# A decoder layer on eight cores: the order of the instructions of every engine made by a model of the engines at build time

One Trainium2 chip, all 8 NeuronCores (two dies of four). The metric is the time of one execution on the device in microseconds (us), of the slowest core. A program on all 8 cores has a second, slower state in some executions, in which the cores of one die show a lower clock. Comparisons below use the fast runs; where a slow run is named, it is called slow.

## The reference

A hybrid decoder layer: two batches of 4096 tokens, 2048 channels. Cut to what the argument touches:

```python
h = rms_norm(x, norm_gain)                       # needs the sum of squares of each token
q, k, v, z_attn, u_pool, z_pool, gates = split(einsum('bsd,de->bse', h, w_in), ...)
q = rms_norm(q.reshape(B, S, 3, 8, 128), q_norm_gain)     # one norm for each head
k = rms_norm(k.reshape(B, S, 3, 8, 128), k_norm_gain)
for g, (window, dilation) in enumerate(((128, 1), (512, 4), (2048, 16))):
    qg, kg = partial_rope(q[:, :, g], pos), partial_rope(k[:, :, g], pos)   # first 32 of 128 channels
    o_g, lse_g = dilated_window_attention(qg, kg, v[:, :, g], window, dilation)
# [cut: mix of the three groups by their softmax denominators]
# [cut: pooling mixer, two sigmoid gates, two branch products]
return x + einsum('bsd,de->bse', merged, w_out)
```

Each core does 1024 tokens of its own and the keys and values of the tokens before them that the third window reaches (the halo). The kernel has these stages: stage 1, keys and values of the third group over all those tokens, in chunks of 512; stage 2, query and key projections with the attention of 24 head-and-group units laid between them; then pooling (stage 3), gates with the branch products, and the output product.

## The kernel before

The program first calls `S.op(engine, instruction, reads, writes)` for everything. Each engine gets its instructions in the order of these calls, and semaphore waits are made from the reads and writes. An engine executes strictly in its order: **what is ready but stands behind something that waits, waits too**. So the order of the calls is the schedule. TensorE's projections are the backbone, and everything else is put in at fixed points of it:

```python
own_q, bg_q, late_q = [], [], []          # norms; attention; second halves of rotations
def tick(kc):                             # called after each of the 16 matmuls of a projection
    if kc in (3, 7, 11, 15):
        pop_own()                         # the next norm or rotation step, if there is one
    elif kc in (1, 5, 9, 13):
        pop_bg()                          # the next attention step, if its time has come

def project(banks, lhs, mov, n, reads):
    i = banks[nxt("pp", len(banks))]      # buffers go round in a fixed order
    pcount[0] += 1
    need(("ps", i))                       # flush what still uses this buffer
    # [cut]
    for kc in range(KC):
        S.op("pe", ...matmul...)
        tick(kc)
    return i
```

The steps themselves: a norm is square (ScalarE), a matmul with ones that sums over the 128 channels (TensorE), logarithm and exponential (ScalarE), product (VectorE). A rotation exchanges two halves of 16 channels by two small DMAs from SBUF to SBUF and then does three short instructions on VectorE, put in a fixed number of projections later:

```python
def rope(tag, rots, B_rots, st, B_st, c0, n, tb, B_tb, t0, after=None, wait=2):
    def swap():
        # [cut] two DMAs on SyncE's queue: rb[32:48] <- st[16:32], rb[48:64] <- st[0:16]
        def turn():
            # [cut] three VectorE instructions of 32 x n elements
        turn.due = pcount[0] + wait       # two projections later, whatever the DMA does
        late_q.append(turn)
    return swap
```

The norm of a chunk of x: 8 squares of 1024 columns (ScalarE), 7 adds and a fold (VectorE), one fp32 matmul that sums the partitions, logarithm and exponential, and 16 scalings (VectorE).

## Time and profile before

| | before |
|---|---|
| median of the first 3 runs | 1870.58 us (1868.52 to 1874.1) |
| TensorE busy | 1600.7 us, 86% of the span, 7774 matmuls |
| ends of stage 1, stage 2, stage 3 (read from the trace) | 513, 1290, 1418 us |
| share of TensorE in the chain of work that ended last | 71% |

"Busy" counts a slow matmul as busy too. So I compare with a floor: each matmul's undisturbed distance from the next (0.216 us for 512 columns, taken from the gate stage where nothing disturbs), summed. Time minus this sum is "lost". The lines of the profile are shown in the prediction and not again here. In all such lines PE is TensorE and PEld its loading of weights, DVE is VectorE, ACT ScalarE, POOL GpSimd and SP SyncE; a q behind the name marks the issue of a DMA, and L12 is line 12 of the kernel. In a list of waits the numbers are us in all, how often, and the longest.

### The profile page before, as it was taken

Reading aid. Unit: us, or ns where it says so; the run is one execution under the profiler, and the core shown is the slowest. Engines: PE = TensorE matmul, PEld = TensorE weight load, DVE = VectorE, ACT = ScalarE, POOL = GpSimd, SP = SyncE. Lnnn points to the kernel's source line nnn. Section 1 sums busy time; section 2 is a strip of 40 time slices with the busy share of each in tenths; the row PEclk is TensorE's granted clock in tenths of the full one; section 3 lists DMA queues with packets and bytes.
Section 4 is the critical chain, followed back from the end, with each engine's and each line's share of the span. In section 5 each row is a group of like instructions: output and inputs, shape, how many; then the busy total and the mean of one; then the engine's idle time right before and its main releaser. Section 6 shows DMA issues by size and latency. Waiting matters only on the chain.

```text
span 1870.6 us, 22928 instructions; the slowest of 8 cores (1861.7 to 1870.6 us)
## 1 busy us (share of the span) xinstructions
PE 1600.7 (86%) x7774; PEld 754.0 (40%) x7774; DVE 698.5 (37%) x1041; ACT 551.2 (29%) x890; POOL 76.1 (4%) x147
## 2 busy tenths in 40 slices
PE   0397778879999787778998788778999999999997
PEld 0143333324644334343453434334444444444443
DVE  2456646472100444453403544545642121112121
ACT  2235344433112444443314444443211111111000
POOL 1000000000000000000000000000000000000000
PEclk9898889889999987898999898888999999999999
DMA  9743514234454232313325323223434444444683
GB/s 202 161 135 89 147 35 123 58 91 87 87 128 66 52 84 37 73 22 79 81 46 92 76 52 74 48 40 60 91 68 75 73 78 79 79 72 76 135 225 113
DMA packets 79027, 163.06 MB, mean 87 GB/s; under 512 B 33664, under 2 KB 41728, under 8 KB 78144
## 3 DMA queue, kind: packets, MB, share of 16 engines
q0 software_dynamic: 20592, 84.42, 26.6%
q1 hardware_dynamic: 57696, 76.72, 13.8%
q8 instruction: 64, 1.05, 0.2%
q10 hardware_dynamic: 624, 0.46, 0.1%
q14 instruction: 51, 0.42, 0.1%
HBM read 220.48 MB, written 20.97 MB: 129 GB/s over the span
## 4 chain that ended last, share of the span: by engine, by line
PE 71%; DVE 10%; DMA 6%; ACT 6%; issue 5%; SPq 1%; DVEq 0%; ACTq 0%
PE ps L476 53%; PE ps L1054 6%; PE ps L1023 6%; DVE s_acc L536 3%; ACT s_sqf L534 2%; DMA s_xs_66<-xc 2%; PE ps L578 2%; DMA s_xs_60<-xc 1%; DVE s_DEN L719 1%; PE ps L798 1%; PE ps L769 1%; PE ps L547 1%; DVE s_NUM L716 1%; DVE s_hTo L557 1%; ACT s_rr_53 L583 1%
## 5 line engine op out<-in xcount | busy, mean ns | idle before, releaser
L476 PE MATMUL ps<-s_hTo,s_w_57 128*128 128x512 bf16 x3328 | 806.3, 392 | 1.1 <-ACT s_ue_115 L945 0.9
L476 PEld LDWEIGHTS ps<-s_hTo,s_w_57 128*128 128x128 bf16 x3328 | 332.4, 101 | 370.1 <-issue 31.0
L476 PE MATMUL ps<-s_hTh_55,s_w_57 128*128 128x512 bf16 (+2 forms) x640 | 116.6, 327 | 16.2 <-DVE s_hTh_55 L557 15.8
L397 POOL DMA_DIRECT2D s_w_57<-wst x136 | 72.2, 535 | 1172.7 <-PE ps L476 920.0
L476 PE MATMUL ps<-s_w_57,s_hTo 128*128 128x512 bf16 x512 | 113.6, 379 | 0.0
L1054 PE MATMUL ps<-s_mT,s_w_57 128*128 128x512 bf16 x512 | 110.7, 379 | 0.0
L536 DVE TENSOR_TENSOR s_acc<-s_acc,s_sqf 128x1024 f32<-128x1024 f32 x49 | 60.0, 1225 | 111.9 <-ACT s_sqf L534 111.9
L476 PEld LDWEIGHTS ps<-s_hTh_55,s_w_57 128*128 128x128 bf16 x640 | 56.2, 105 | 76.4 <-issue 35.4
L594 ACT ACTIVATE s_sq_50<-ps 128x512 bf16<-128x512 f32 (+1 forms) x72 | 40.3, 560 | 142.8 <-PE ps L476 142.8
L578 PE MATMUL ps<-s_sq_51,s_ones 128*128 128x512 bf16 x72 | 29.1, 404 | 59.3 <-ACT s_sq_51 L594 59.3
L476 PEld LDWEIGHTS ps<-s_w_57,s_hTo 128*128 128x128 bf16 x512 | 54.0, 106 | 54.4
L1054 PEld LDWEIGHTS ps<-s_mT,s_w_57 128*128 128x128 bf16 x512 | 50.1, 98 | 60.4
L585 DVE SCALAR_TENSOR_TENSOR s_kS_97<-ps,s_cst,s_rr_52 128x128 bf16<-128x128 f32 (+1 forms) x8 | 4.4, 551 | 173.3 <-ACT s_rr_52 L583 173.3
L476 PE MATMUL ps<-s_hTh_56,s_w_57 128*128 128x512 bf16 x256 | 64.1, 406 | 0.0
L581 ACT ACTIVATE s_rr_52<-ps 128x512 f32<-128x512 f32 (+1 forms) x72 | 40.3, 560 | 75.9 <-PE ps L578 66.3
L581 ACT ACTIVATE s_rr_53<-ps 128x512 f32<-128x512 f32 x72 | 43.1, 599 | 64.9 <-PE ps L578 54.0
L476 PE MATMUL ps<-s_w_58,s_hTh_56 128*128 128x512 bf16 x256 | 61.5, 403 | 0.0
L1023 PE MATMUL ps<-s_aT,s_w_57 128*128 128x512 bf16 x256 | 60.5, 379 | 0.0
L1023 PE MATMUL ps<-s_pT,s_w_57 128*128 128x512 bf16 x256 | 60.5, 379 | 0.0
L547 PE MATMUL ps<-s_acc,s_onesf 128*128 128x512 f32 x14 | 14.2, 1114 | 53.2 <-DVE s_acc L542 53.2
L476 PE MATMUL ps<-s_w_58,s_hTh_55 128*128 128x512 bf16 x256 | 55.9, 379 | 0.0
L476 PE MATMUL ps<-s_w_58,s_hTo 128*128 128x512 bf16 x256 | 55.6, 379 | 0.0
(319 smaller groups left out, 1576.0 us busy)
## 6 DMA issues: line engine op xcount, KB each, us to landing
s_w_57<-wst POOLq DMA_DIRECT2D x136, 512.0 KB, 5.2
s_w_57<-wst POOLq DMA_DIRECT2D x4, 2048.0 KB, 16.1
s_w_58<-wst POOLq DMA_DIRECT2D x2, 2048.0 KB, 61.3
s_xs_59<-xc SPq DMA_DIRECT2D x7, 512.0 KB, 5.2
s_xs_60<-xc SPq DMA_DIRECT2D x7, 512.0 KB, 5.3
s_xs_61<-xc SPq DMA_DIRECT2D x6, 512.0 KB, 7.7
s_xs_62<-xc SPq DMA_DIRECT2D x6, 512.0 KB, 6.3
s_xs_63<-xc SPq DMA_DIRECT2D x6, 512.0 KB, 4.4
```

Source lines behind the costliest of these rows:

```text
L397: S.op("pool", lambda g: g.dma_start(out=t[:].rearrange("p k n -> p (k n)"), in_=wst[row]), writes=bufs, dsem=f"w{i}")
L476: S.op("pe", lambda t, kc=kc, a=lhs(kc), b=mov(kc): t.matmul(ps[i][:, 0:n], lhsT=a, rhs=b, start=(kc == 0), stop=(kc == KC - 1)), reads=re ...
L534: S.op("act", lambda a: a.activation(out=sqf[:], in_=xv, func=AF.Square), reads=[B_xs[i]], writes=[B_sqf])
L536: S.op("dve", lambda v: v.tensor_tensor(out=acc[:], in0=acc[:], in1=sqf[:], op=ALU.add), reads=[B_acc, B_sqf], writes=[B_acc])
L547: S.op("pe", lambda t: t.matmul(ps[AUX][:], lhsT=onesf[:], rhs=acc[:, 0:512], start=True, stop=True), reads=[B_acc, B_onesf], writes=[B_ps ...
L557: S.op("dve", lambda v: v.scalar_tensor_tensor(out=dst(kc), in0=xs[i][:, kc % 2, :], scalar=gsc[:, kc:kc + 1], in1=rsb[ri][:], op0=ALU.mul ...
L578: S.op("pe", lambda t: t.matmul(ps[AUX][:, 0:n], lhsT=ones[:], rhs=sq[si][:, 0:n], start=True, stop=True), reads=[B_sq[si], B_ones], write ...
L581: S.op("act", lambda a: a.activation(out=rr[ri][:, 0:n], in_=ps[AUX][:, 0:n], func=AF.Ln, bias=float(128 * EPS)), reads=[B_ps[AUX]], write ...
L583: S.op("act", lambda a: a.activation(out=rr[ri][:, 0:n], in_=rr[ri][:, 0:n], func=AF.Exp, scale=-0.5), reads=[B_rr[ri]], writes=[B_rr[ri]])
L594: S.op("act", lambda a: a.activation(out=sq[si][:, 0:n], in_=ps[i][:, 0:n], func=AF.Square), reads=[B_ps[i]], writes=[B_sq[si]])
L1023: S.op("pe", lambda t, yi=yi, h=h, m=m, w=w, which=which, src=src: t.matmul(ps[yi][:], lhsT=w[:, 8 * which + h, :], rhs=src[:, h, 512 * m: ...
L1054: S.op("pe", lambda t, fi=fi, db=db, m=m, w=w: t.matmul(ps[fi][:], lhsT=w[:, db, :], rhs=mT[:, db, 512 * m:512 * m + 512], start=(db == 0) ...
```

## The change

Intent: no fixed points, and hardly any fixed turns of buffers (blocks of weights and pieces of x still go round). Each piece of work (a norm, a rotation, a bank of attention, a load) becomes a process that asks for buffers from counted pools and yields instructions, each with a duration. A discrete-event model of the five engines runs the processes at build time; when an engine is free, it takes the ready instruction with the highest priority. The sequence that comes out is frozen in the program.

The core of the diff (names kept, long runs cut):

```diff
-        own_q, bg_q, late_q = [], [], []
-        def tick(kc):
-            if kc in (3, 7, 11, 15):
-                pop_own()
-            elif kc in (1, 5, 9, 13):
-                pop_bg()
+class Flow:
+    LAT = {"pe": 0.5, "act": 0.2, "dve": 0.2, "pool": 0.3, "sp": 0.2}   # the model's us from another engine's result to its use on this one
+    RATE = 0.31e6                                                       # the model's bytes per us of large DMAs
+    def dispatch(self, eng):
+        if self.busy[eng] or not self.pend[eng]:
+            return
+        _, _, p, dur, fn, reads, writes, dma = heapq.heappop(self.pend[eng])   # by priority
+        self.S.op(eng, fn, reads=reads, writes=writes, ...)                    # the order is fixed here
+        done = self.t + dur
+        # [cut]
+        if dma is not None:
+            size = dma[0]
+            if size >= 200e3:
+                start = max(done + 1.5, self.dma_free)
+                self.dma_free = start + size / self.RATE
+                land = self.dma_free + 0.7
+            else:
+                land = done + 4.0                  # in the model a small DMA: 4 us, whatever else is under way
+def act_us(n):
+    return 0.16 + n * 0.00087
+def dve_us(n, cheap=False):
+    return 0.15 + n * (0.00053 if cheap else 0.00105)
```

```diff
-        def norm_stage(i, n, si, gcol, dst, B_dst, r=1): ...
+        def norm(i, n, gcol, dst, B_dst, r=1):
+            si = yield ("acq", P_sq)
+            yield ("op", "act", act_us(n), ...square..., [B_ps[i]], [B_sq[si]])
+            ax = yield ("acq", P_aux)
+            yield ("op", "pe", mm_us(n), ...matmul with ones..., [B_sq[si], B_ones], [B_ps[ax]])
+            F.release(P_sq, si)
+            # [cut] logarithm, exponential, product; then the buffers are released
```

Work moves as well. From the second chunk on the adds of squares go to GpSimd; the first weights wait until part of x has landed; and the late tokens that stage 2 needs are copied out of the normed chunks instead of being loaded and normed as a chunk of their own:

```diff
+                if k < 2:                                     # a load of weights
+                    yield ("wait", E_x[(0, 3 + 3 * k)])
+                    first = [B_xs[3 + 3 * k]]                 # a dependence, so a semaphore wait on the chip
+                if k == 8:                                    # the first load of value weights
+                    yield ("wait", E_x[(1, 7)])               # of the model only: no dependence
+                eng, dur = ("dve", dve_us(1024)) if c == 0 else ("pool", 2.4)     # adds of squares
+        def late_copy(c):
+            src = hTh[hi][:].rearrange("p k (r l) -> p k r l", r=4)[:, :, :, 96:128]
+            dst = hX[:, :, 0:LATE].rearrange("p k (l r) -> p k r l", r=16)[:, :, 4 * c:4 * c + 4, :]
+            yield ("op", "pool", 4.0, lambda g: g.tensor_copy(out=dst, in_=src), ...)
```

## The prediction

> **What bounds the kernel now.** I read the busy table and the slices first, then the stages, then what TensorE waited for, then single places in order of time. The slices of the page:
>
> ```profile
> PE   0397778879999787778998788778999999999997
> PEclk9898889889999987898999898888999999999999
> DMA  9743514234454232313325323223434444444683
> ```
>
> TensorE is the engine that matters, but only the right third of its row (gates, branch products, output projection) is full. The left two thirds are at 7 or 8 tenths, with a granted clock of 8 or 9 tenths. The same by stage (columns: stretch, its length, busy time and count of TensorE, weight loads, VectorE, ScalarE, GpSimd, granted clock, DMA share, GB/s):
>
> ```profile
> 0.00:43.10 43.10, 0.00 (x0) 0.00 (x0) 9.91 (x13) 9.62 (x9) 5.63 (x14) 1.00 0.95 203
> 43.10:93.00 49.90, 17.41 (x45) 5.89 (x46) 22.78 (x26) 12.88 (x16) 0.00 (x0) 0.87 0.75 165
> 93.00:513.00 420.00, 359.49 (x1547) 167.00 (x1546) 204.06 (x326) 157.93 (x237) 1.06 (x2) 0.92 0.36 95
> 589.00:900.00 311.00, 251.01 (x1300) 120.61 (x1298) 142.91 (x217) 132.81 (x228) 10.16 (x20) 0.88 0.31 61
> 980.00:1290.00 310.00, 249.32 (x1330) 121.03 (x1327) 146.95 (x224) 135.84 (x235) 14.85 (x28) 0.90 0.33 63
> 1418.00:1749.50 331.50, 331.50 (x1537) 150.29 (x1536) 66.16 (x96) 44.22 (x65) 25.45 (x48) 1.00 0.44 77
> ```
>
> The last line is the yardstick: 1537 matmuls of 512 columns in 331.5 us are 0.216 us each, no gap, full clock. I counted every matmul by width and gave each its undisturbed distance (0.216 us for 512 columns, in proportion below that, 0.03 us at least). This gives 1505 us for the whole kernel. So 366 us of 1870.6 are lost, by subtraction in each stretch: 43 before the first matmul; 38 to 93 us; 80 in the rest of stage 1 (key and value projections of all tokens, to 513 us); 191 in stage 2 (attention, 513 to 1290), of which 122 are gaps and the rest slow matmuls and short waits; 4 in the pooling stage; none in the gates; 11 at the end. In stage 2 most 512-column matmuls lie 0.22 us apart, but 174 lie 0.42 us apart, all after a gap.
>
> What TensorE waited for:
>
> ```profile
> PE ps L798 <- DVE s_E_107 L776: 70.6, 16, 7.3
> PE ps L578 <- ACT s_sq_51 L594: 59.3, 21, 8.7
> PE ps L547 <- DVE s_acc L542: 53.2, 7, 43.1
> PE ps L578 <- ACT s_sq_50 L594: 30.8, 6, 11.6
> ```
>
> These are not slow producers: VectorE and ScalarE are under half busy in the stages concerned. They stand in the wrong order. One place shows it (the first two lines VectorE, the last TensorE):
>
> ```profile
> 622.15 0.94 DVE L611 TENSOR_TENSOR s_kS_99<-s_kS_99,s_tabb 32x1536 bf16<-32x1536 bf16 x1 [4.11 <-DMA s_rotb_105<-s_kS_99]
> 625.39 0.41 DVE L776 TENSOR_TENSOR s_E_107<-s_E_107,s_msk 128x512 bf16<-128x512 bf16 x1
> 625.94 0.58 PE L798 MATMUL ps<-s_E_107,s_vS_91 128*128 128x256 bf16 x3 [7.25 <-DVE s_E_107 L776]
> ```
>
> The exponentials of this bank ended at 617.6 us. The mask multiplication (L776) stands behind a rotation that waits 4.1 us for its DMA, so TensorE waits 7.25 us for a 0.41 us instruction with ready inputs. In stage 1 it is ScalarE: squares of the next chunk, waiting for x, stand before the squares of a norm.
>
> [...]from 1420 to 1750 us all eight cores run dense at 1.00. Hence I charge a denser kernel no clock. [...]the trace shows 322 GB/s when x alone is loading (75 to 80 us).
>
> **The change part by part.** The arithmetic stays. Four things move.
>
> *1. Order.* Each piece of work is now a process that asks for buffers by count. A model with durations for each instruction issues the highest-priority ready one, and that sequence is frozen. I use none of its times, only the order that it leaves. Its durations are sound against the trace: ScalarE at 512 columns 0.605 us (trace 0.60), mask 0.42 (0.41), norm product 0.76 (0.75), rotation DMAs 4 us after issue (trace about 1.9 unobstructed, so generous). Its handoffs are too short from TensorE (0.2[...]) and too long towards it (0.5, 0.14). The chain last matmul, square, norm matmul is 1.305 us in the model[...]. Before, four matmuls (0.86 us) were put between; in the new TensorE order it is 1.3 to 1.5 us of work in most of the 96 norms of stage 2. So a norm should wait 0 to 0.3 us, not up to 9. The rotations no longer stand before ready masks, because the order counts the DMA.
>
> *2. First chunk.* Weights wait until part of x has landed. 4.2 MB at 320 GB/s are 13 us; with the start and the first weight's share, I put the last piece of x at 19 us (trace before: 39.8, with weights competing). The same tail as before (square 1.1, add 1.2, column sum, here twice and 4.1, logarithm and exponential 1.3, handoffs) puts the first scaled block at 27 us instead of 46.7. Three heads follow block by block instead of waiting for all 16: done at about 42; the other five (17.3 us) at 59.
>
> *3. Second chunk.* The sum of squares moves to GpSimd, with one buffer for the squares[...]. In the GpSimd order these adds stand behind the copy of the late tokens, which needs chunk 0 fully scaled (41 us). So about 45, [...]fold, sum and roots to 76, scaling 76 to 89, keys of chunk 1 done near 115. TensorE needs 62 us for what it has done by then: 53 us lost[...]. That compares with 43+38 plus later waits. For later chunks a cycle of about 40 us lies beside 55 us of projections, so it is hidden.
>
> *4. Smaller.* The seventh chunk (512 late tokens) is copied from the halo instead: 8 loads, 8 squares (8.5 us ScalarE), adds (9.3 us) and 16 scalings (13 us) of VectorE go, all beside other work. The 16-column and 128-column pieces become 352 and 384: 3 us off the floor, 1502.
>
> Sum: 1502 floor; 56 to the end of chunk 1's keys; 4 in the rest of stage 1; stage 2: 25, chosen as 96 norms at 0.1 to 0.2 us plus a few pile-ups on the three projection banks (a bank's next turn comes 6.9 us, two projections, after its own ends[...]); pooling 3; end 11. **1601 us, so I say 1600**, a saving of 270: 100 in stage 1 and 166 in stage 2.
>
> **The rivals.** *GpSimd becomes the bound of stage 1.* For: [...]it also issues all weight loads. [...]If an add took 5 us, chunks would come every 58 us and stage 1 would lose about 30 more: 1630. *The frozen order meets other times than the model's*, and in-order engines stall at each wrong guess, as they do now. [...]Against: [...]there is generous slack on DMAs. With half of the old gaps left, stage 2 loses 80: 1655. *ScalarE or VectorE becomes the bound of stage 2.* Each is busy near 143 us of 311; squeezed into 225 us that is 64%, so local queues but no bound: 15 more, 1615. *All goes perfectly*: 1565.
>
> **Range and chances.** 1565 is the floor with only the start and the end lost; 1650 takes two rivals at half size each or the second nearly whole. For a change within 2% some 230 us of the 270 would have to fail to come; no rival reaches that. 98% faster by over 2%, 1.2% within, 0.8% slower.
>
> **What would show it.** First matmul of a projection near 28 us, stage 1 ending near 412 instead of 513; TensorE at 9 tenths from about 115 us on; granted clock 0.97 or more in stage 2, no wait there over 3 us repeated per head; gates and output unchanged at 331 and 121 us. Wrong if the adds on GpSimd exceed 4 us, if waits for squares or masks keep tens of us, or if the dense attention stage on all cores lowers the granted clock.

With all terms the sum came to 1601 us; its 56 us to the end of the second chunk's keys were the 53 of step 3 and a cut term of 3 for slow matmuls after the wait. Cut in step 3 is the length of an add on GpSimd, which no run had shown; the times from 76 us on, the 53 us, and the cycle of 40 us behind the "4 in the rest of stage 1" rested on it, and stay as my estimates. Cut in step 1 is the handoff from TensorE to ScalarE, which I had too long: in the trace before, a norm's square starts 0.48 us after the start of the projection's last matmul (median of the 105 that waited for it), so 0.26 us after its 0.216 us, and the chain to the norm matmul is 0.26 + 0.60 + 0.14, about 1.0 us. The 0 to 0.3 us a norm and the 25 us of stage 2 were chosen with a longer chain and stay as my estimates too.

## The result, and the profile after

The changed kernel takes 1629.36 us (median of 4 runs, 1628.61 to 1689.09; the kernel before in the same rounds 1871.93, 1868.52 to 1874.1). The longest run is slow: one die at a clock near 0.94. The ratio is 0.8704, with an interval of 0.8689 to 0.8719. A ratio is the mean time of one kernel's fast runs over the mean of the other's fast runs of the same rounds, so it is not quite the ratio of the medians quoted. The outputs are correct.

The slices of the page of the changed kernel, the profiled core being core 1 with a span of 1627.1 us:

```profile
PE   2638999899999999989999999999999999999997
PEclk9859999999999999999999999999999999999999
DMA  9951544114443644343343443445344444444883
```

From the fifth slice on, TensorE is full or nearly so, at 9 tenths of the clock or more. Most of what is left to lose is in the first four slices, 163 us. In the chain of work that ended last TensorE has 85% instead of 71%. The same by stage (stretch, its length, busy time and count of TensorE, weight loads, VectorE, ScalarE, GpSimd, granted clock, DMA share, GB/s): to the first scaled block, to the second chunk's keys, to the end of stage 1, part of stage 2, and the gates.

```profile
0.00:32.90 32.90, 3.75 (x4) 1.17 (x4) 9.22 (x13) 10.96 (x11) 4.58 (x12) 1.00 0.91 199
32.90:106.50 73.60, 33.91 (x138) 14.16 (x138) 35.02 (x50) 22.06 (x34) 27.79 (x11) 0.74 0.74 161
106.50:456.30 349.80, 328.63 (x1456) 156.17 (x1457) 163.24 (x239) 133.10 (x207) 100.70 (x37) 0.96 0.37 98
490.00:800.00 310.00, 303.80 (x1757) 160.71 (x1756) 154.50 (x236) 151.04 (x263) 13.97 (x27) 0.99 0.42 83
1181.00:1511.00 330.00, 330.00 (x1531) 149.61 (x1529) 66.86 (x97) 43.31 (x63) 25.34 (x48) 1.00 0.45 77
```

The stretch of stage 2 holds 1757 matmuls in 310 us where before there were 1300 in 311, with a clock of 0.99 instead of 0.88. The gates are what they were. The second line is the sore place: 73.6 us with 33.9 us of TensorE in them. The waits of TensorE (in all, how often, the longest) say by what:

```profile
PE ps L742 <- ACT s_sq_50 L739: 44.6, 5, 23.5
PE ps L669 <- DVE s_acc L660: 27.6, 1, 27.6
PE ps L669 <- POOL s_acc L664: 10.0, 2, 9.7
PE ps L1067 <- DVE s_qS_100 L777: 6.2, 1, 6.2
```

The masks (70.6 us before) have gone from the list. The squares of norms (59.3 and 30.8 before) keep 44.6 us, but in 5 waits of stage 1 instead of 27 all over the kernel. Where the loss lies, over the whole of both kernels (my sums over all matmul records of the profiled core, core 2 before and core 1 after, by the floor described above; the floor is 1505.0 before and 1502.3 after):

| lost by TensorE, us | to 120 us | 120 to 460 us | 460 us to the last matmul | sum |
|---|---|---|---|---|
| before | 82.8 | 78.1 | 193.7 | 354.6 |
| after | 80.9 | 21.6 | 11.0 | 113.5 |

**So the first 120 us gave next to nothing net**: by the same sums the eight cores lose 80 to 83 us there before and 77 to 81 after. The first projection starts at 33.9 us instead of 61.0, but nearly all of these 27 us are given back by 120 us. The gain is 56 us in the rest of stage 1 and 183 us behind it. With 11.3 us from the last matmul's start to the end, 1502.3 + 113.5 + 11.3 is the span of 1627.1.

Three places of stage 1 make up most of the loss after. *First*, the first chunk's squares: one buffer takes them to the adds, so ScalarE (1.06 us) and VectorE (1.23) take turns, 2.48 us a step, and the last add ends at 27.5 us.

*Second*, at 68 us TensorE waits 23.5 us. From the timeline of the changed kernel (start, length, engine, line; in brackets the idle time before and what ended it):

```profile
59.77 1.11 POOL L587 DMA_DIRECT2D s_w_57<-wst  x2
64.25 1.26 SPq L764 DMA_DIRECT2D s_rota_76<-s_kst_72  x2
...
88.45 0.41 DVE L773 TENSOR_TENSOR s_kst_72<-s_kst_72,s_tabh_79 32x512 bf16<-32x512 bf16 x1 [19.99 <-DMA s_rota_76<-s_kst_72]
...
90.56 0.60 ACT L746 ACTIVATE s_rr_51<-ps 128x512 f32<-128x512 f32 x1 [21.51 <-DVE s_kst_69 L751]
...
91.79 0.58 PE L742 MATMUL ps<-s_sq_50,s_ones 128*128 128x512 bf16 x1 [23.47 <-ACT s_sq_50 L739]
```

GpSimd issues the two loads of value weights at 59.8 us. The exchange for one head's rotation is issued 4.5 us later and does not land; VectorE stands at that rotation, ScalarE's logarithm waits for VectorE to free a buffer, and the square that TensorE waits for stands behind the logarithm. The square is what the list of waits names; the DMA is what held it up. The list of DMA issues in the stretch from 58 to 92 us gives the size of each and the time from issue to landing:

```profile
s_w_57<-wst POOLq DMA_DIRECT2D x2, 2048.0 KB, 23.2
s_rota_76<-s_kst_72 SPq DMA_DIRECT2D x2, 16.0 KB, 22.6
s_rota_77<-s_kst_69 SPq DMA_DIRECT2D x2, 16.0 KB, 1.8
```

The same 16 KB take 22.6 us beside the value weights and 1.8 us after them. In that stretch the weights' queue moved 4.19 MB in 288 packets and the exchanges' queue 0.65 MB in 766; how the two share the DMA engines was not shown. The second chunk's x was not in the way: its last piece had landed at 59.2 us. The build-time model gives every small DMA 4.0 us.

*Third*, the copy of late tokens. At the fourth of the four:

```profile
278.42 8.95 POOL L717 COPY s_hX<-s_hTh_55 128x2048 bf16<-128x2048 bf16 x1 [3.92 <-DVE s_hTh_55 L695]
...
278.64 8.44 DVE L775 TENSOR_TENSOR s_rota_78<-s_rota_78,s_tabh_80 32x512 bf16<-32x512 bf16 x1
...
293.58 0.58 PE L742 MATMUL ps<-s_sq_50,s_ones 128*128 128x512 bf16 x1 [8.10 <-ACT s_sq_50 L739]
```

The copy takes 8.95 us where the model has 4.0, and a rotation step of 0.41 us on VectorE that starts 0.2 us later takes 8.44 us and ends within 0.3 us of the copy's end. The 110 rotation steps of stage 1 that have no GpSimd work beside them all took 0.42 us or less; the 34 that have some took 43.8 us more than that together. The norm's product, which has one input in PSUM, takes a median of 0.751 us in stage 1 both alone (34 of them) and beside GpSimd (14).

### The profile page after: what moved, and what is told of

Same layout as the page of the kernel before. It is cut to its first block, busy times and chain, and to the rows that moved or that the text cites. A ratio compares the mean times of both kernels' runs of the same rounds, so it can differ in the third digit from the quotient of the medians.

```text
span 1627.1 us, 22823 instructions; the slowest of 8 cores (1618.4 to 1627.1 us)
## 1 busy us (share of the span) xinstructions
PE 1519.9 (93%) x7774; PEld 751.7 (46%) x7774; DVE 663.1 (41%) x976; ACT 531.4 (33%) x880; POOL 202.2 (12%) x191
## 3 DMA queue, kind: packets, MB, share of 16 engines
q8 instruction: 65, 1.06, 0.3%
## 4 chain that ended last, share of the span: by engine, by line
PE 85%; DMA 4%; DVE 3%; issue 2%; POOL 2%; ACT 2%; SPq 0%; ACTq 0%; DVEq 0%; POOLq 0%
PE ps L725 64%; PE ps L1431 7%; PE ps L1381 7%; POOL s_acc L660 2%; DMA s_rota_76<-s_kst_72 2%; PE ps L742 2%; PE ps L1067 2%; PE ps L1102 1%; DMA s_xs_59<-xc 1%; ACT s_sqf L658 1%; PE ps L1106 1%; PE ps L848 1%; DMA s_rotb_101<-s_qS_100 1%; DVE s_rota_78 L775 1%; DMA s_rota_76<-s_kst_69 1%
## 5 line engine op out<-in xcount | busy, mean ns | idle before, releaser
L725 PE MATMUL ps<-s_hX,s_w_56 128*128 128x512 bf16 (+3 forms) x3712 | 799.4, 367 | 0.0
L725 PEld LDWEIGHTS ps<-s_hX,s_w_56 128*128 128x128 bf16 x3712 | 363.6, 98 | 373.5 <-issue 3.5
L725 PE MATMUL ps<-s_w_56,s_hX 128*128 128x512 bf16 x672 | 147.2, 379 | 0.0
L725 PEld LDWEIGHTS ps<-s_w_56,s_hX 128*128 128x128 bf16 x672 | 71.6, 107 | 71.5
L660 POOL TENSOR_TENSOR s_acc<-s_acc,s_sqf 128x1024 f32<-128x1024 f32 x35 | 85.9, 2455 | 127.6 <-ACT s_sqf L658 127.6
L746 ACT ACTIVATE s_rr_51<-ps 128x512 f32<-128x512 f32 (+1 forms) x72 | 41.4, 576 | 103.6 <-PE ps L742 69.9
L725 PE MATMUL ps<-s_hTh_55,s_w_56 128*128 128x512 bf16 x256 | 66.7, 406 | 3.6 <-DVE s_hTh_55 L695 2.4
L742 PE MATMUL ps<-s_sq_50,s_ones 128*128 128x512 bf16 (+1 forms) x72 | 27.7, 384 | 44.6 <-ACT s_sq_50 L739 44.6
L746 ACT ACTIVATE s_rr_52<-ps 128x512 f32<-128x512 f32 (+1 forms) x72 | 42.3, 588 | 66.3 <-PE ps L742 61.5
L739 ACT ACTIVATE s_sq_49<-ps 128x512 bf16<-128x512 f32 (+1 forms) x72 | 41.1, 570 | 56.9 <-PE ps L725 42.9
L725 PE MATMUL ps<-s_w_57,s_hTh_54 128*128 128x512 bf16 x256 | 57.7, 384 | 0.0
L725 PE MATMUL ps<-s_w_57,s_hTh_55 128*128 128x512 bf16 x256 | 55.9, 379 | 0.0
L725 PE MATMUL ps<-s_w_57,s_hX 128*128 128x512 bf16 x256 | 55.6, 379 | 0.0
L739 ACT ACTIVATE s_sq_50<-ps 128x512 bf16<-128x512 f32 (+1 forms) x72 | 41.8, 580 | 34.2 <-PE ps L725 33.4
L725 PE MATMUL ps<-s_hTh_54,s_w_56 128*128 128x512 bf16 x208 | 47.0, 379 | 0.0
L749 ACT ACTIVATE s_rr_52<-s_rr_52 128x512 f32<-128x512 f32 (+1 forms) x72 | 44.5, 618 | 6.6 <-ACT s_rr_52 L746 0.7
```

The lines of the kernel that those rows point to most:

```text
L660: yield ("op", eng, dur, lambda v: v.tensor_tensor(out=acc[:], in0=acc[:], in1=sqf[:], op=ALU.add), [B_acc, B_sqf], [B_acc])
L725: yield ("op", "pe", mm_us(n), lambda t, kc=kc, a=lhs(kc), b=rhs(kc): t.matmul(ps[i][:, 0:n], lhsT=a, rhs=b, start=(kc == 0), stop=(kc == ...
L739: yield ("op", "act", act_us(n), lambda a: a.activation(out=sq[si][:, 0:n], in_=ps[i][:, 0:n], func=AF.Square), [B_ps[i]], [B_sq[si]])
L742: yield ("op", "pe", mm_us(n), lambda t: t.matmul(ps[ax][:, 0:n], lhsT=ones[:], rhs=sq[si][:, 0:n], start=True, stop=True), [B_sq[si], B_o ...
L746: yield ("op", "act", act_us(n), lambda a: a.activation(out=rr[ri][:, 0:n], in_=ps[ax][:, 0:n], func=AF.Ln, bias=float(128 * EPS)), [B_ps[ ...
L749: yield ("op", "act", act_us(n), lambda a: a.activation(out=rr[ri][:, 0:n], in_=rr[ri][:, 0:n], func=AF.Exp, scale=-0.5), [B_rr[ri]], [B_r ...
```

## The experiments

Twelve kernels ran, all with correct outputs, in three groups, each group on one chip. The kernel before ran beside them: 1879.56, 1901.25 and 1893.74 us median, so the second and third groups saw more disturbed runs of it. The third group ran on another chip than the first two and has no run of the changed kernel, so a difference of a few us from it is not certain there. For differences of a per cent I therefore read the fast runs themselves and, in each profiled run, the losses of core 1 by the method of the table above, all of it:

| kernel | fast runs, us (how many) | ratio to before | lost to 120 | 120 to 460 | after 460 |
|---|---|---|---|---|---|
| changed kernel | 1628.6 to 1629.5 (3) | 0.8704 | 80.9 | 21.6 | 11.0 |
| value weights later | 1616.2 to 1635.7 (4) | 0.8618 | 61.1 | 28.3 | 9.9 |
| copy on ScalarE | 1626.0 to 1647.2 (4) | 0.8681 | 88.8 | 12.7 | 9.4 |
| model without durations | 1997.4 to 2001.0 (4) | 1.0622 | 74.5 | 117.1 | 289.3 |
| copy modelled at 9 us | 1608.8 to 1612.4 (5) | 0.8521 | 80.0 | 3.0 | 10.4 |
| copy in other order | 1611.9 to 1612.2 (3) | 0.8528 | 78.0 | 5.5 | 9.0 |
| three mends | 1610.1 to 1627.9 (6) | 0.8523 | 63.5 | 24.3 | 8.4 |
| adds on VectorE | 1624.8 to 1625.1 (2) | 0.8612 | 78.9 | 19.7 | 8.4 |
| mends, adds on VectorE | 1608.0 to 1609.5 (2) | 0.8526 | 83.2 | 0.0 | 9.6 |
| model 1.4 times as long | 1668.8 to 1670.3 (4) | 0.8851 | 81.6 | 23.0 | 43.9 |

A loss counts where it begins: the copy on ScalarE has a wait of 8.1 us from 120 to 128 us that stands in "to 120" for this reason, and is otherwise like the changed kernel. Some runs counted as fast have two neighbouring cores about 18 to 25 us longer at a clock near 0.96 (the 1627.9, 1635.7 and 1647.2 here); I do not read differences from their times. Two of them were profiled, but core 1 was not among the slow cores (clock 0.977 and 0.979).

### What carries the gain: the model without durations

```diff
-    LAT = {"pe": 0.5, "act": 0.2, "dve": 0.2, "pool": 0.3, "sp": 0.2}
+    LAT = {"pe": 0.0, "act": 0.0, "dve": 0.0, "pool": 0.0, "sp": 0.0}
+        if eng != "pe" and dma is None:
+            dur *= 0.02
```

> Changed kernel with a model that knows no durations but those of TensorE and the DMAs: the other engines' instructions last 2% and handoffs nothing. Buffers, banks, pieces and priorities are the same. Theory (the gain of the attention stage is the order that the durations give): norm matmuls and score products come right behind their producers in TensorE's order, TensorE waits at each, the attention stage loses 80 us or more again, 1720 or more. Rival (counted buffers, finer dependencies and free priorities carry the gain): 1660 or less.

1997.65 us (1997.4 to 2001.03), a ratio of 1.0622 (1.0582 to 1.0661): slower than the kernel before, with the processes, the counted buffers and the priorities of the changed one. The waits of TensorE on core 1:

```profile
PE ps L744 <- ACT s_sq L741: 117.4, 141, 9.3
PE ps L671 <- POOL s_acc L666: 82.2, 5, 29.0
PE ps L1069 <- DVE s_qS L779: 40.6, 12, 9.2
```

A model that thinks a square is ready at once puts the matmul of the norm directly behind it, 141 times. So buffers and priorities alone do not make the gain; it needs the durations. How much counted buffers, or the copy in place of a seventh chunk, add to a timed order is not shown: no kernel was run with a timed order and without them.

### How exact the durations must be

```diff
+        if eng != "pe" and dma is None:
+            dur *= 1.4
```

> The changed kernel with every duration of VectorE, ScalarE and GpSimd in the build-time model 1.4 times as long; the latencies, the DMA and TensorE as they are. It asks how exact the model must be. Theory A (an order made with too long durations only keeps more distance between a result and its use, and stage 2 has enough buffers for that): within 15 us of the changed kernel, stage 2 within 8 us. Rival B (in-order engines are stalled by each wrong guess): 40 us or more slower, with waits for squares and masks spread over stage 2.

1670.17 us, a ratio of 0.8851 (0.8808 to 0.8894), about 41 us more than the changed kernel. 33 of the 35 us that core 1 loses more lie after 460 us, where waits for masks and for squares are back:

```profile
PE ps L744 <- ACT s_sq L741: 45.6, 13, 17.6
...
PE ps L1104 <- DVE s_E L1074: 12.9, 4, 4.2
```

This is the rival's side of the line, just. A model whose durations of VectorE, ScalarE and GpSimd are all 40% too long gives back a sixth of the gain; it does not ruin it.

### The fixed scheme with better constants

```diff
-            if kc in (3, 7, 11, 15):
+            if kc in (6, 9, 12, 15):
-            elif kc in (1, 5, 9, 13):
+            elif kc in (1, 5, 8, 13):
-        def rope(..., after=None, wait=2):
+        def rope(..., after=None, wait=3):
```

> The kernel before with two constants of its fixed scheme changed: the norm matmul stands 7 instead of 4 matmuls into the next projection, and the turn of a rotation may come 3 instead of 2 projections after its DMAs. Theory (fixed points fail because the queues of the in-order engines differ from place to place): a small part of the gain, 1870 -> 1830 or more. Rival (the old scheme only had badly chosen constants): 1780 or less.

1859.02 us, a ratio of 0.988 (0.9842 to 0.9918). Later points leave a norm more time and the rotations a longer distance from their DMAs, and give 1.2% of the 13%. I tried one set of constants, so this does not show that no fixed points could do better.

### The first chunk's loads alone, in the kernel before

```diff
+                first = [B_xs[3 + 3 * row]] if row < 2 else []      # the first two weights wait for x
-        prefetch(16)
         for j in range(8):
             x_load(0, j)
+        prefetch(16)
```

> The kernel before, with one idea of the change alone: the first chunk of x is loaded before the first weights, which wait until part of it has landed. Theory A (the start gains from the order of loads, whatever makes the order of instructions): the first matmul of a projection comes near 33 us instead of 46.7 and the whole is 8 to 20 us faster, that is a ratio of 0.989 to 0.996. Rival B (the fixed insertion points give the time back at the next wait, which here is for the second chunk's squares): the ratio is within 0.003 of 1.

The two fast runs took 1872.26 and 1880.2 us; the ratio of 0.9944 (0.9869 to 1.0019) fits both theories. The trace tells more. TensorE, core 1:

```profile
44.24 6.63 PE L477 MATMUL ps<-s_hTh,s_w 128*128 128x512 bf16 x20 [15.78 <-DVE s_hTh L558]
62.87 0.58 PE L579 MATMUL ps<-s_sq,s_ones 128*128 128x512 bf16 x1 [12.00 <-ACT s_sq L595]
...
85.19 0.58 PE L579 MATMUL ps<-s_sq,s_ones 128*128 128x512 bf16 x1 [17.12 <-ACT s_sq L595]
```

The first projection starts at 44.2 us instead of 61.0 (later than the 33 that I expected, since in this kernel it waits for all 16 scaled blocks). By 120 us only 5.7 of these 16.8 us are left (77.1 us lost against 82.8 on core 2 of the kernel before; on the same core 1 about 3 are left): the waits for squares at 63 and 85 us are 12.0 and 17.1 us where they had been 11.6 and 4.4. Ahead of both, ScalarE stood idle 12.5 and 13.4 us until a piece of the second chunk's x had landed, and the norm's square stood behind that. So a kernel that starts earlier waits longer for the next chunk. The changed kernel loses its earlier start in the second chunk too, though by another wait.

### The value weights later

```diff
                 if k == 8:
-                    yield ("wait", E_x[(1, 7)])
+                    yield ("wait", E_rs[1])
```

> Changed kernel, but the two value-weight loads (8 MB of source) wait until the sum of squares of chunk 1 is done. Theory (these loads fill the DMA engines while the rotation DMAs of chunk 0 are out; one of those took 23 us and held VectorE, ScalarE and TensorE): the rotation DMA lands in about 2 us, the 23.5 us wait of TensorE at 68 us goes, time 1629 -> about 1606. Rival (the loads are needed by then anyway): the value projections wait for their weights instead, time 1625 to 1635.

1616.79 us, a ratio of 0.8618 (0.8548 to 0.8687). On core 1, TensorE, GpSimd's issue of the value weights, and the exchanges between 58 and 92 us (size, us from issue to landing):

```profile
72.57 0.58 PE L742 MATMUL ps<-s_sq,s_ones 128*128 128x512 bf16 x1 [5.47 <-ACT s_sq L739]
82.52 1.11 POOL L587 DMA_DIRECT2D s_w<-wst  x2
s_rota<-s_kst SPq DMA_DIRECT2D x10, 16.0 KB, 1.8
```

The value weights were issued at 82.5 us instead of 59.8. The wait of 23.5 us at 68 us became 5.5 us, and the exchanges took a median of 1.8 us. The wait of 9.7 us for the second chunk's adds stayed, and between 120 and 460 us 7 us more were lost. So the value weights were the cause of the long wait, and of the 20 us that went before 120 us about 12 to 14 reach the end.

### The copy: by engine, by model, by pattern

First the engine, with the copy in four pieces on ScalarE:

```diff
-            yield ("op", "pool", 4.0, lambda g: g.tensor_copy(out=dst, in_=src), B_hTh[hi], [B_late[c]])
+            for q in range(4):
+                yield ("op", "act", 0.65, lambda a, q=q: a.copy(out=dst[:, 4*q:4*q+4], in_=src[:, 4*q:4*q+4]), ...)
```

> Changed kernel, but the copy of the late tokens is four pieces on ScalarE instead of one 8.9 us copy on GpSimd. Theory (the copy, in the model 4.0 us, stands before the adds on GpSimd and stretches a VectorE rotation beside it to 8.4 us; three waits of TensorE of 4 to 8 us come of it): these three waits go, 1629 -> about 1611. Rival (the waits move to ScalarE, which gets 10 us more work in stage 1, or the 23 us wait at the start covers it all): 1625 to 1635.

1626.92 us, a ratio of 0.8681 (0.8593 to 0.8769): no gain to speak of, as the rival said. The group of these pieces on ScalarE (count, busy time, mean ns of one):

```profile
L718 ACT COPY s_hX<-s_hTh 128x512 bf16<-128x512 bf16 x16 | 37.8, 2360 | 3.7 <-DVE s_hTh L695 3.3
```

Four times 2.36 us are 9.4 us for a chunk, as slow as on GpSimd. My idea that the copy was slow because GpSimd is fell. What both have in common is the pattern: the writes lie 32 bytes apart. So the other order, four neighbouring elements at a time:

```diff
-            src = ....rearrange("p k (r l) -> p k r l", r=4)[:, :, :, 96:128]
-            dst = ....rearrange("p k (l r) -> p k r l", r=16)[:, :, 4 * c:4 * c + 4, :]
+            src = ....rearrange("p k (r l) -> p k l r", r=4)[:, :, 96:128, :]
+            dst = ....rearrange("p k (l r) -> p k l r", r=16)[:, :, :, 4 * c:4 * c + 4]
```

> The copy of late tokens walks its tile in another order (four neighbouring elements of the destination at a time, instead of elements 32 bytes apart); same elements, same engine, same place. On ScalarE the copy had taken as long as on GpSimd, so the pattern of addresses is suspected. Theory A (the pattern of the writes sets the copy's duration): a copy falls from 8.9 us to under 5, the stretched VectorE instruction beside it (8.4 us) falls too, the waits behind the copies go, and the time falls by 10 to 18 us. Rival B (the number of elements, or the strided reads, set it): 8 us or more for a copy, and the time within 4 us.

The copy, on GpSimd as in the changed kernel (count, minimum, median and maximum in ns, first and last start):

```profile
L717 POOL COPY s_hX<-s_hTh x4: 3745/3767/3822, 41.7 to 264.0; 128x2048 bf16<-128x2048 bf16 x4
```

3.77 us instead of 8.94, for the same elements on the same engine. The fast runs take 1611.9 to 1612.2 us, and the loss between 120 and 460 us falls from 21.6 to 5.5. The pattern is settled as the cause of the copy's duration, and it is that of the writes: the reads went the other way, from neighbouring elements to elements 256 bytes apart. Why writes 32 bytes apart take longer was not shown, and I tried no other strides.

Is it the copy's duration that costs, or the model's error about it? Only the number in the model changed here; the copy stays at 9 us:

```diff
-            yield ("op", "pool", 4.0, lambda g: g.tensor_copy(out=dst, in_=src), ...)
+            yield ("op", "pool", 9.0, lambda g: g.tensor_copy(out=dst, in_=src), ...)
```

> Only the duration that the build-time model has for the copy of late tokens is changed, from 4.0 to 9.0 us, near the 8.9 that the trace shows; every instruction stays, only the order may move. Theory A (the copy costs time because the model has its duration wrong, and puts what depends on it too early): the three waits of 7, 4 and 8 us behind the copies shrink to under 3 us each, 8 to 14 us less in all. Rival B (the copy costs time because it holds up GpSimd and, beside it, VectorE, in whatever order): the waits stay within 3 us of what they are and the time is within 3 us.

> The changed kernel once more, as the base of the three others on the same chip. Theory and rival expect the same: 1629 us, with its waits of 23.5 us at 68 us, 9.7 us at 97 us, and 7, 4 and 8 us behind the three copies of late tokens, so that the last chunk of keys and values ends near 456 us.

The changed kernel again took 1630.3 us in its undisturbed runs. With the true number in the model: 1608.8 to 1612.4 us, a ratio of 0.8521 (0.849 to 0.8552), and 3.0 us lost between 120 and 460 us where it was 21.6. The copy still takes 8.99 us, and stretched rotations still cost VectorE 44.9 us in stage 1, but nothing on the path. The list of waits of core 1 has no more of the copies' waits in it:

```profile
PE ps L742 <- ACT s_sq L739: 27.5, 5, 23.8
PE ps L669 <- DVE s_acc L660: 25.4, 1, 25.4
PE ps L669 <- POOL s_acc L664: 12.9, 2, 9.7
```

The gain is larger than the 8 to 14 us expected. One constant is worth 18 to 20 us, 1.2%: as much as a copy that is really fast. What cost time was that the order did not know.

### Three mends together

```diff
-                    yield ("wait", E_x[(1, 7)])        # value weights
+                    yield ("wait", E_rs[1])
-        sqf = one("sqf", [128, 1024], F32);  acc = one("acc", [128, 1024], F32)
+        sqf = many("sqf", 2, [128, 512], F32);  acc = one("acc", [128, 512], F32)
+        # [cut] 15 adds of 512 columns a chunk (GpSimd from the second chunk on), no fold
+        # and the copy's other order, as above
```

> Three mends together: the value weights wait until the second chunk's scaling, the squares of a chunk come in halves of 512 with two buffers so that ScalarE's next square runs beside the add, and the copy walks in the other order. Theory (the 44 us by which stage 1 missed my sum are these three): the first scaled block comes near 28 us instead of 32.9, the second chunk's keys start near 82 us instead of 106, the copies cost less than 5 us in all, stage 1 ends near 415 to 425 us instead of 456 and the whole takes 1590 to 1600 us. Rival (what is taken away in one place comes back in the next wait, because the loads and the chain of adds are the bound there): stage 1 ends at 440 us or later and the whole takes 1610 us or more, no better than with the deferred weights alone (1616.8).

The sum matmul of the first chunk starts at 24.0 us instead of 27.6 and the first projection at 29.0 instead of 33.9, as hoped. But the fast runs take 1610.1 to 1611.6 (one disturbed at 1627.9), no better than the copy's other order alone: the rival's side, which said 1610 us or more. The 63.5 us lost by 120 us are a gain of 17, and 24.3 us go between 120 and 460 us, where the copy's mend alone loses 5.5. Two of the new waits of core 1 can be named. At 121 us TensorE waits 6.6 us for a square behind a rotation: the value weights, now issued at 76 us, and the next chunk's x are loading until then (from 81 to 122 us the DMA row stands at 8 or 9 tenths in most slices), and between 75 and 122 us an exchange took a median of 12.2 us. At 177 us it waits 4.3 us for the adds on GpSimd, which come in 15 halves of 1.26 us with 0.20 us between instead of 7 of 2.46 on the mean. What was taken away came back, as the rival said; for the adds' part I suspected that GpSimd's adds stretch VectorE's rotation steps, and the next two runs test that.

### The adds back on VectorE

In the changed kernel, alone:

```diff
-                eng, dur = ("dve", dve_us(1024)) if c == 0 else ("pool", 2.4)
+                eng, dur = ("dve", dve_us(1024))
```

> One part of the change undone: the adds of the squares stay on VectorE in every chunk, in an order that the same model makes with VectorE's durations. Theory A (moving the adds to GpSimd cost more than it gave: an add takes 2.46 us there against 1.23[...]): the wait of 9.7 us for the second chunk's adds falls under 3 us, the rotations of stage 1 come back to 0.41 us except beside the copies, and the whole is 5 to 15 us faster than the changed kernel. Rival B (VectorE has no room in stage 1, so adds that wait for x hold up the norms and rotations, as in the kernel before): 5 us or more slower.

The rotation steps: the 34 beside GpSimd work cost VectorE 43.8 us in the changed kernel, 8.0 of it beside the copy.

The fast runs take 1624.8 and 1625.1 us, 4 us less than the changed kernel (whose repeat ran on another chip), and the losses between 120 and 460 us are the same within 2 us (19.7 and 21.6). So the adds on GpSimd neither cost nor give much there, and that theory fell in the main: VectorE's lost time was off the path. Now the adds are what the copy holds up, on VectorE in core 1:

```profile
198.47 8.92 DVE L660 TENSOR_TENSOR s_acc<-s_acc,s_sqf 128x1024 f32<-128x1024 f32 x1 [0.59 <-ACT s_sqf L658]
```

And at 65 us TensorE waited 23.7 us, again behind a rotation whose exchange took 27.2 us beside the value weights (and the end of x), which are now issued at 52.2 us. Why they come earlier is plainest in the last run.

All mends, with the adds on VectorE:

```diff
     # as in the three mends, and
-            eng, dur = ("dve", dve_us(512)) if c == 0 else ("pool", 1.25)
+            eng, dur = ("dve", dve_us(512))
```

> The three mends of the kernel before last (value weights later, squares in halves with two buffers, copy in the other order), and the adds on VectorE as well. That kernel gave only 20 us where its parts alone gave 12 and 18, and its new waits stood where GpSimd's adds ran beside rotations of VectorE. Theory A (the adds on GpSimd are what took the rest back): the waits of 6 and 5 us for squares and adds at 63 and 71 us go below 3 us each, stage 1 gains 8 to 20 us over that kernel, and the whole takes 1585 to 1600 us. Rival B (the loads of x and of the weights set these waits): the whole stays at 1603 to 1615 us.

1608.0 and 1609.5 us in the fast runs: the time that the second theory gave, and, as it turns out, its cause too, the loads. Of the first theory one part came: between 120 and 460 us core 1 lost nothing. But one wait of 32.3 us at 59 us takes the gain:

```profile
PE ps L743 <- ACT s_sq L740: 36.2, 3, 32.3
```

The DMA issues between 42 and 86 us on core 1 (size, us from issue to landing):

```profile
s_w<-wst POOLq DMA_DIRECT2D x2, 2048.0 KB, 29.7
...
s_rota<-s_kst SPq DMA_DIRECT2D x6, 16.0 KB, 36.5
```

and GpSimd's timeline:

```profile
42.13 1.06 POOL L587 DMA_DIRECT2D s_w<-wst  x2
```

The value weights were not held back at all. x came late beside them as well (its last piece landed at 82.8 us, at 59.2 in the changed kernel), and x stands before the exchanges: x and the exchanges both go through SyncE's queue; the pieces of the second chunk's x were issued there by 38.4 us, and the six exchanges, issued from 44.8 us on, landed one after the other from 82.9 to 83.7. So here the exchanges came behind x on their own queue, and x came late beside the weights; exchanges on another queue were not tried. `yield ("wait", E_rs[1])` is a wait in the model; on the chip it is only a place in GpSimd's order. With the adds on GpSimd, that place lay behind them and so the load really came late (59.8 us in the changed kernel, 75.9 us with the three mends). With the adds gone, GpSimd has nothing to do between the first copy and this issue, and issues it at 42.1 us. What holds a load back must be a dependence, as it is for the first two weights. A kernel with such a dependence and the adds on VectorE was not run; from core 1's losses of 61.1 us to 120 us (value weights later) in place of 83.2, an estimate for core 1 is 1604.7 - 22 = 1583 us. It stays an estimate.

Best of the runs: the fast ones of the copy modelled at 9 us and of the mends with the adds on VectorE, near 1610 us, are 1.2% under the changed kernel.

## Why the prediction was right, and where it was not

The time was right in its range: 1600 said, 1629 measured, 1565 to 1650 given. **The mechanism was right:** engines stood in the wrong order, not short of capacity. Stage 2 lost nearly all of its waits, and the model without durations shows that it is the timed order that does it. But that the sum came within 2% is partly luck, as errors of opposite sign partly cancel. Told by the terms of the sum, with the measured value from core 1:

| term | said | measured |
|---|---|---|
| floor | 1502 | 1502.3 |
| lost to the end of the second chunk's keys | 56 | 80.9 (to 120 us) |
| rest of stage 1 | 4 | 21.6 |
| stage 2 and pooling | 25 + 3 | 11.0 |
| end | 11 | 11.3 |
| sum | 1601 | 1627.1 |

**Step 1, order: right, and mis-sized by 17 us to the good.** I chose 0.1 to 0.2 us for each of 96 norms and a few pile-ups. The trace has almost no such waits: 11.0 us in all after 460 us, of which one rotation's DMA is 6.2. The model's handoff from TensorE (0.2 us) that I called too short is near the trace's 0.26 us. The masks' wait of 70.6 us went to nothing, as the step said. The rival of a frozen order that meets other times did not come in stage 2, but the run with durations 1.4 times too long shows that it is real: 33 us more lost after 460 us. In stage 1 it did come, and made most of what I missed: the exchange (22.6 us against the model's 4.0) and the copy (8.9 against 4.0). My "generous slack on DMAs" was wrong there.

**Step 2, first chunk: mis-sized by 6 us, and its gain did not stay.** The first scaled block came at 32.9 us, not 27. I took "the same tail as before" for the squares: they are paced at 2.48 us by one buffer, so seven more steps follow the first square at 8.4 us. The halves with two buffers bring the first projection forward by 4.9 us, to 29.0. And a start that is 27 us earlier left 2 us by 120 us. The experiment that puts x first in the kernel before shows the same: of 16.8 us, 5.7 are left. I had added the start's gain to the sum as though it could not be given back; the next chunk's chain sets the time there.

**Step 3, second chunk: the step that failed.** I wrote that roots would be done at 76 and scaling run to 89. They were delayed by the wait that I did not see: rotations behind the value weights, 23.5 us at 68 us, and behind it 9.7 us for the adds; the second chunk's keys started at 106.5 us. I had the DMA of a rotation at "about 1.9 us unobstructed" and called the model's 4 us generous. It is, unobstructed. With the value weights held back by GpSimd's order the wait is 5.5 us. An add on GpSimd took a median of 2.35 us and a mean of 2.46, near the model's 2.4.

**Step 4, smaller: the copy was not smaller.** I put it at some 4 us (41 to 45 in step 3), without a row to take it from, and called the new work hidden. It took 8.9 us, and the "4 in the rest of stage 1" became 21.6. The runs name the part of it: 18 of them go when the model is told the true duration.

**The rivals.** GpSimd as the bound of stage 1 did not come: the kernel with the adds on VectorE is 4 us faster only. But the price of GpSimd's work that I did not count, VectorE's stretched rotation steps, is 43.8 us of VectorE in stage 1. It stays off the path as long as the order has slack. No rival of mine named the DMA queues.

**The clock.** I charged nothing for a denser kernel, and in fast runs that held: a mean of 0.97 on the profiled core against 0.94 before, and 1.00 in the gates. In slow runs it is lower: one slow run of the three mends has the cores of one die at 0.81 to 0.82 and 1884 to 1889 us, with the other die at 0.98 and 1603 to 1608 us. So it is a state of some executions here, not of the load alone. The 174 slow matmuls of stage 2 before the change stand after gaps of very different length: by the last gap before them (of 0.4 us or more), 126 follow one of over 3 us and 48 one of 0.6 to 2.9 us.

**What was to show it:** the first projection near 28 us (33.9), stage 1 ending near 412 (456), TensorE at 9 tenths from 115 us (from about 120), no wait over 3 us repeated per head in stage 2 (right), gates unchanged (330 us for 1531 matmuls, right), granted clock of 0.97 or more in stage 2 (0.99, right). One sign of being wrong did come: waits for squares kept 44.6 us. They stand in stage 1 alone, behind one exchange and three copies, and not all over the order as before.

## What to carry to other kernels

An order made by a timed model is as good as its durations: without them it was slower than the fixed scheme, and with three engines' durations 40% too long it gave back a sixth of the gain. So look for the one instruction or transfer whose measured time is twice the model's, since it alone can cost a per cent. For the copy, telling the model was as good as making the thing fast; a model that knows how slow the exchanges are beside large loads was not tried. A wait in a model of the order is no wait on the chip (the load that it should hold back was issued at 42.1 us): what must come late needs a dependence. And a gain at the start is only a gain if the chain of the next chunk comes earlier too.
